# One hybrid recurrent and mixture-of-experts block: conditioning work dealt out anew, a norm in columns, other rounds of experts

## The chip, the cores and the metric

The kernel runs as one program on one core of a Trainium2 chip. A time is the device time of one execution in microseconds; where several were timed, the median stands. A profiled execution also gives a trace, whose times count from its first instruction (its span). In the trace PE is the matrix engine (PEld its weight loads), DVE the vector engine, ACT the scalar engine, POOL the general engine, and SP the engine whose queue issues the large loads. L12 is line 12 of the kernel's file.

## The reference, cut to what matters

One layer for 256 tokens of width 2048. A conditioning vector c gives six rows of 2048 (shift, scale and gate for each half), all by one product with w_ada:

```
mod = silu(c) @ w_ada + b_ada                       # (2048) x (2048, 12288), f32: 100 MB
sh1, sc1, g1, sh2, sc2, g2 = split(mod, 6)
x = x + g1 * mixer(rmsnorm(x) * (1 + sc1) + sh1)    # w_in 2048 x 6152, w_out 2048 x 2048
x = x + g2 * moe(rmsnorm(x) * (1 + sc2) + sh2)      # top 2 of 32 experts, each 3 x 4 MB
y = rmsnorm(x) * final_g
```

In the mixer, four mLSTM heads stand beside eight blocks of a linear recurrence. The recurrence's output `yr` is normed over each block of 128 channels: `yr * rsqrt(mean(yr*yr) + eps) * lru_norm_g`. In the experts' half a router picks a group and two experts for each token; each expert has a gate, an up and a down matrix of 4 MB each in f32. With the inputs that are timed, 512 places (256 tokens, two experts each) fall very unevenly on the experts: the fullest has 66, and six of the 32 have none, so that 26 experts are loaded, 312 chunks of 1 MB.

## The kernel before, in words

All weights stream through a ring of seven buffers of 1 MB (`ring`; one buffer of 128 partitions x 8 KB is a chunk). The function `chunk` takes the next buffer and issues its load on SP's queue. SP's and PE's instructions stand in the order in which the code is written; those of DVE and ACT are placed by a scheduler. A load into a buffer waits until the last reader of the buffer's former content is done.

The program has these stages. First two sections of the conditioning (`ada_now`) with the first products of w_in, then the remaining groups of w_in (`w_in_group`, for the gates, queries, keys, values and outputs), then w_out by token, then the routing, then the experts in ten rounds (`experts`), and an output stage. A product of w_in or w_out splits each chunk on ACT and DVE (`split`) into a high and a low part and multiplies in three passes on PE.

The four later sections of the conditioning (2, 4, 3 and 5, in this order, 16 chunks each) are read beside w_in and w_out. `between()` runs after each chunk of w_in and w_out: it takes one step of the side work and one more chunk of `ada_later`, sometimes two. The last six of the 64 chunks are read in the routing (`fill`). Each chunk is either multiplied on PE into the section's sum in PSUM, or multiplied and added on DVE into the tile `acc` (two instructions of 128 x 1024). `ON_PE` says which: of the sections 2, 4 and 3 the first three chunks, of section 5 all 16, 25 in total. `ada_sum` ends a section: PE adds up `acc` over its partitions (four products, 128 x 512 each), DVE adds the bias row.

The norm of the recurrence (`lru_norm`) squares on ACT, sums with a matrix of ones on PE, so that the sum stands in all 128 partitions, takes the root on ACT and the reciprocal on DVE over 128 x 512 elements, four times.

The experts' rounds: PE works with four column tiles of 32 tokens at once. An entry `(rank, tiles)` of `ROUNDS` is one expert, by its rank in fullness (30 and 31 are experts 0 and 1, known before the routing), and how many of the four tiles it takes. A round of two experts reads 24 chunks, one of four reads 48. PE does the same number of products in both. The loads of an expert without tokens are skipped, but its chunks still take their buffers in the ring. The ranks 24 and 25 have no tokens with these inputs. While the experts run, the ring has six more buffers, cut from tiles that are done with. The very first of them stands in the place of `acc`:

```
if count[0] in (1, 7):
    tag, bufs = ("acc", 1) if count[0] == 1 else ("ws", 3)
    ring.appendleft(st([128, 4, 512], f"more{count[0]}", tag, bufs))
```

So the first chunk of the first expert goes into `more1`, the old `acc`. Behind round `OVER_AFTER` (counted from 0) stands a loop for overfull experts (`overflow`). With these inputs it runs no times, but every engine meets at it; eight chunks of the next round are issued ahead of it (`PREFETCH`).

Of the kernel before, what the change touches and what calls it, by code (L numbers as in the profile page):

```python
# [13 lines left out]
AF = mybir.ActivationFunctionType  # L14
OP = mybir.AluOpType
# [3 lines left out]
S = 256  # L19
# [8 lines left out]

ROUNDS = [[(30, 2), (31, 2)], [(0, 3), (7, 1)], [(8, 1), (9, 1), (10, 1), (11, 1)], [(1, 3), (12, 1)],
          [(13, 1), (14, 1), (15, 1), (16, 1)], [(2, 3), (17, 1)], [(18, 1), (19, 1), (20, 1), (21, 1)],
          [(3, 2), (4, 2)], [(22, 1), (23, 1), (24, 1), (25, 1)], [(5, 2), (6, 2)]]
LAST = [26, 27, 28, 29]

OVER = [(30, 2), (31, 2), (0, 2), (1, 2), (2, 2)] + [(r, 1) for r in range(3, 15)]
CAP = {rank: 32 * tiles for members in ROUNDS for rank, tiles in members}
NR = len(ROUNDS)
NB = 1 + sum(n for _, n in OVER)
OVER_AFTER = 2  # L40

FILL = 3

# [1 line left out]

BESIDE = 53

ON_PE = {2: 3, 4: 3, 3: 3, 5: 16}

PREFETCH = 8  # L50

# [13 lines left out]
def constants():  # L65
# [20 lines left out]
    base, cap, osh = np.zeros(32), np.zeros(32), np.zeros(32)  # L86
    for r, members in enumerate(ROUNDS):
        col = 0
# [19 lines left out]
def block_kernel(ctx, tc, x, c, w_ada, b_ada, w_in, b_gates, vec_a, vec_b, w_lru_a, w_lru_x, w_out,  # L108
                 w_rt, b_rt, w_e_gate, w_e_up, w_e_down, const, out):
    nc = tc.nc  # L110
    V, A, G, PE, SP = nc.vector, nc.scalar, nc.gpsimd, nc.tensor, nc.sync
# [8 lines left out]
    def pb(shape=(128, 512), name="pb"):  # L120
        return psum.tile(list(shape), F32, name=name, tag="b", bufs=2)

    def w2(shape, name, dt=F32):
        return sb.tile(list(shape), dt, name=name, tag="w2", bufs=8)

    def st(shape, name, tag=None, bufs=1, dt=F32):
        return sb.tile(list(shape), dt, name=name, tag=tag or name, bufs=bufs)
# [4 lines left out]
    def tcopy(o, i):  # L132
        V.tensor_copy(o, i)
# [33 lines left out]
    ones = cs[:, C_ONE:C_ONE + 128]  # L167
# [31 lines left out]
    eps = epsc[:, 0:1]  # L199
# [6 lines left out]
    cz = st([128, 16, 36], "cz")  # L206
    V.memset(cz, 0.0)
    V.tensor_scalar(cz[:, :, 3], th, 0.5, None, op0=OP.mult)
    oz = cs[:, C_SEL + 8:C_SEL + 44]
    ada = st([128, 6, 16], "ada")  # L210
# [28 lines left out]

    acc = st([128, 4, 512], "acc")  # L240

    def ada_sum(sec, ps):
        yield
        if ON_PE[sec] < 16:
            for n in range(4):
                PE.matmul(ps[32 * n:32 * n + 32], oz[:, 3:35], acc[:, n], start=False, stop=True, skip_group_check=True)
        row = w2([128, 512], "row")
        V.tensor_tensor(row, ps, arow[sec], op=OP.add)
        yield
        one = 1.0 if sec in (1, 4) else 0.0  # L250
        for o, perm in ((ada[:, sec], False),) + (((adx[:, sec - 3], True),) if sec in (3, 4) else ()):
            pc = pb([128, 4, 4])
            for j in range(4):
                PE.matmul(pc[:, :, j], row[:, j::4] if perm else row[:, j * 128:j * 128 + 128],
                          ident[:, 0:128:32], start=True, stop=True)
            V.tensor_scalar(o, pc.rearrange("p a b -> p (a b)"), one, None, op0=OP.add)
            yield

    def ada_later():

        for sec in (2, 4, 3, 5):
            ada_start(sec, 32)
            ps = pa()
            pe = ON_PE[sec]
            for k in range(16):
                w = ada_row(sec, k)
                if k < pe:
                    for n in range(4):  # L270
                        PE.matmul(ps[32 * n:32 * n + 32], cz[:, k, 3:35], w[:, n], start=k == 0, stop=k == 15,
                                  skip_group_check=True)
                else:
                    for h in range(0, 4, 2):
                        o = acc[:, h:h + 2]
                        if k == pe:
                            V.tensor_scalar(o, w[:, h:h + 2], cz[:, k, 3:4], None, op0=OP.mult)
                        else:
                            V.scalar_tensor_tensor(o, w[:, h:h + 2], cz[:, k, 3:4], o, op0=OP.mult, op1=OP.add)  # L279
                if k == 15:  # L280
                    sums.append(ada_sum(sec, ps))
                yield

    later = ada_later()

    def bcast(cols):
        p = pb([128, 4, 128])
        for j in range(4):
            PE.transpose(p[:, j], cols[:, j:j + 1].to_broadcast([128, 128]), ident)  # L289
        return p.rearrange("p a b -> p (a b)")  # L290
# [46 lines left out]
    lng = lambda ch: col[:, 128 + ch:129 + ch]  # L337
# [178 lines left out]
    def lru_norm():  # L516
        sq = []
        for pair in range(4):
            a = XR[:, 2 * pair:2 * pair + 2]
            V.tensor_tensor(a, a, GR[:, 2 * pair:2 * pair + 2], op=OP.mult)  # L520
            sq.append(w2([128, 512], "sq"))
            A.activation(sq[-1], a.rearrange("p a b -> p (a b)"), AF.Square)
        yield
        for pair in range(4):
            pq = pb()
            PE.matmul(pq, ones, sq[pair], start=True, stop=True)
            A.activation(sq[pair], pq, AF.Sqrt, scale=1.0 / 128, bias=eps)
        yield
        for pair in range(4):
            V.reciprocal(sq[pair], sq[pair])  # L530
            for i, n in enumerate((2 * pair, 2 * pair + 1)):
                V.scalar_tensor_tensor(GR[:, n], XR[:, n], lng(n), sq[pair][:, i * S:i * S + S], op0=OP.mult, op1=OP.mult)
            yield

    def evac_qk(which, g):
# [29 lines left out]
    def values(hd):  # L565
        P = PT[hd]
        for t in range(2):
            po = pb([128, 257])
            for h in range(t + 1):
                lh = P[:, t * 128:t * 128 + 128] if h == 0 else P[:, 256:]  # L570
                PE.matmul(po, lh, va_aug[:, h, hd], start=h == 0, stop=h == t)
            i = hd * 2 + t
            tcopy(HR[:, t, hd], po[:, :256])
            tcopy(dn[:, 0, i:i + 1], po[:, 256:257])
            j = w2([128, 256], "tj")
            A.activation(j, HR[:, t, hd], AF.Square, accum_out=dn[:, 1, i:i + 1])
            tcopy(dn[:, 2, i:i + 1], gcols[:, 1, t, hd:hd + 1])
        yield
        if hd < 3:
            return  # L580
        V.tensor_scalar(dn[:, 3], dn[:, 0], -1.0, None, op0=OP.mult)
        V.tensor_tensor(dn[:, 0], dn[:, 0], dn[:, 3], op=OP.max)
        V.tensor_tensor(dn[:, 0], dn[:, 0], dn[:, 2], op=OP.max)
        V.reciprocal(dn[:, 0], dn[:, 0])
        V.tensor_tensor(dn[:, 1], dn[:, 1], dn[:, 0], op=OP.mult)
        V.tensor_tensor(dn[:, 1], dn[:, 1], dn[:, 0], op=OP.mult)
        A.activation(dn[:, 1], dn[:, 1], AF.Sqrt, scale=1.0 / 256, bias=eps)
        V.reciprocal(dn[:, 1], dn[:, 1])
        V.tensor_tensor(dn[:, 0], dn[:, 0], dn[:, 1], op=OP.mult)
        for i in range(8):  # L590
            V.tensor_scalar(HR[:, i % 2, i // 2], HR[:, i % 2, i // 2], dn[:, 0, i:i + 1], None, op0=OP.mult)
# [20 lines left out]
    for sec in (1, 0):  # L612
        ps = pb()
# [51 lines left out]
    XR, GR = XG[:, 0], XG[:, 1]  # L665
# [16 lines left out]
    for g in range(2):  # L682
        ps = [pa() for _ in range(2)]
        for kk in range(4):
            w = chunk(w_in[kk * 512:kk * 512 + 512, 2048 + g * 512:2560 + g * 512]
                      .rearrange("(k p) n -> p k n", p=128))
# [4 lines left out]
    HR = XR.rearrange("p (t h a) s -> p t h (a s)", t=2, h=4)  # L691
# [38 lines left out]
    def router(n):  # L730
        yield
        xts = []
        for i in range(2):
            p = pb([128, 2, S])
            xt = w2([128, 2, S], "xt")
            k = n * 4 + i * 2
            for j in range(2):
                for h in range(2):
                    PE.transpose(p[:, j, h * 128:h * 128 + 128], X1[:, h, (k + j) * 128:(k + j + 1) * 128], ident)
            V.tensor_tensor(xt, p, ada[:, 4, k:k + 2, None].to_broadcast([128, 2, S]), op=OP.mult)  # L740
            xts.append(xt)
            yield
        for i in range(2):
            for j in range(2):
                k = n * 4 + i * 2 + j
                for h in range(2):
                    PE.matmul(plg[:, h], xts[i][:, j, h * 128:h * 128 + 128], wr[:, k], start=k == 0 and h == 0,
                              stop=k == 15, skip_group_check=True)
# [18 lines left out]
    ps = [[pa() for _ in range(2)] for _ in range(2)]  # L767
# [14 lines left out]
    for n in (2, 3):  # L782
        ps = [pa() for _ in range(2)]
# [326 lines left out]
    def members_of(r):  # L1110
        ms, c0 = [], 0
        for rank, tiles in ROUNDS[r]:
            if rank >= 30:
# [94 lines left out]
    for r in range(NR):  # L1208
# [8 lines left out]
        if not last:  # L1217
            Cw = spread_of(r + 1)
            ms = members_of(r + 1)
        if r == OVER_AFTER:  # L1220
            flush()
# [57 lines left out]
```

## Time and profile before

| | |
|---|---|
| median of three runs | 1365.17 us (1364.59 to 1368.4) |
| profiled execution: its own time, its span | 1366.29 us, 1364.4 us |
| PE busy | 1179.1 us (86%) |
| DVE busy | 553.5 us (41%) |
| ACT busy | 348.1 us (26%) |
| moved on SP's queue (q1) | 500.11 MB, 91.8% of 16 engines' span |
| mean granted TensorE clock | 0.956 |

The profiled execution took 1.1 us longer than the median; 1.9 us of its own time lie outside its span. A share over the whole span mixes stages with different limits, so stages are read one by one below. The DMA share of a stretch is the mean busy share of the core's 16 DMA engines.

### The profile page before, as it was taken

The page shows a single profiled execution, that of the slowest core. Times are in us where ns is not written, and L with a number is a line of the kernel's source. Part 1 is how long each engine was busy: PE and PEld are TensorE (multiplying, and loading weights), DVE is VectorE, ACT ScalarE, POOL GpSimd, SP SyncE. Part 2 cuts the span into 40 slices and gives each one's busy share as a digit, 9 for nine tenths or more (in the row PEclk, how much of TensorE's full clock was granted, in tenths as well). Part 3 has the DMA queues.
Part 4 walks back from the last instruction along what each step waited for, and adds up shares of the span by engine and source line. Part 5 has one row for each costly group of instructions (what it writes and reads, how often), then busy time and mean ns, then how long its engine had stood idle before and what let it go on. Part 6 is the DMA issues. An engine that isn't in the chain of part 4 may idle for free. (4 is left out here: it accounts for less than half of the span.)

```text
span 1364.4 us, 20209 instructions
## 1 busy us (share of the span) xinstructions
PE 1179.1 (86%) x8178; PEld 674.6 (49%) x8178; DVE 553.5 (41%) x999; ACT 348.1 (26%) x543; POOL 3.5 (0%) x10
## 2 busy tenths in 40 slices
PE   4888999899999999899987859867789777989986
PEld 0567888788789777534421313313134113343432
DVE  1333679989859943523230130310122201313314
ACT  2332595635435423421100100100001001010103
POOL 0000000000000000000000000000000000000000
PEclk9999999999999999799998989998899888999998
DMA  9999768778969966999999999999999999999995
GB/s 340 367 374 362 260 255 328 281 265 342 387 244 364 388 256 254 414 364 394 424 424 424 424 391 374 424 425 425 425 425 425 425 425 424 425 424 418 365 420 224
DMA packets 116896, 504.82 MB, mean 370 GB/s; under 512 B 12424, under 2 KB 14760, under 8 KB 69184
## 3 DMA queue, kind: packets, MB, share of 16 engines
q1 hardware_dynamic: 115264, 500.11, 91.8%
q0 software_dynamic: 288, 2.10, 0.4%
q8 instruction: 65, 1.06, 0.3%
q10 hardware_dynamic: 1248, 1.29, 0.3%
q14 instruction: 31, 0.25, 0.0%
HBM read 526.54 MB, written 2.10 MB: 387 GB/s over the span
## 5 line engine op out<-in xcount | busy, mean ns | idle before, releaser
L1026 PE MATMUL pa<-ring,XE 128*32 128x512 f32 x1336 | 269.4, 632 | 41.6 <-DMA ring<-in_w_e_up_dram 26.5
L1026 PE MATMUL pa<-more,XE 128*32 128x512 f32 x1224 | 235.1, 632 | 42.5 <-DMA more<-in_w_e_up_dram 23.0
L434 PE MATMUL pa<-HH,ws 128*128 128x256 f32 x640 | 185.7, 290 | 10.7 <-DVE ws L417 10.7
L432 PE MATMUL pa<-HH,ws 128*128 128x256 f32 x640 | 188.5, 295 | 3.6 <-ACT ws L416 1.9
L433 PE MATMUL pa<-HL,ws 128*128 128x256 f32 x640 | 185.1, 289 | 1.4 <-DVE HL L327 1.4
L416 ACT ACTIVATE ws<-ring 128x1024 fp32r<-128x1024 f32 x128 | 134.6, 1059 | 185.3 <-PE pa L434 94.7
L417 DVE TENSOR_TENSOR ws<-ring,ws 128x1024 fp32r<-128x1024 f32 x128 | 154.4, 1218 | 58.2 <-ACT ws L416 57.6
L1026 PEld LDWEIGHTS pa<-ring,XE 128*32 128x32 f32 x1336 | 66.4, 114 | 172.1 <-issue 89.5
L432 PEld LDWEIGHTS pa<-HH,ws 128*128 128x128 f32 x640 | 126.4, 198 | 15.8 <-issue 6.5
L1026 PEld LDWEIGHTS pa<-more,XE 128*32 128x32 f32 x1224 | 57.5, 115 | 153.0 <-issue 82.5
L434 PEld LDWEIGHTS pa<-HH,ws 128*128 128x128 f32 x640 | 126.4, 197 | 12.7 <-DVE ws L417 12.6
L433 PEld LDWEIGHTS pa<-HL,ws 128*128 128x128 f32 x640 | 126.6, 198 | 2.3 <-DVE HL L327 1.9
L1081 PE MATMUL pa<-ring,hT 128*32 128x512 f32 x616 | 110.5, 607 | 11.4 <-DMA ring<-in_w_e_down_dram 11.4
L897 ACT ACTIVATE XE<-pb,adx 128x128 f32<-128x128 f32 x80 | 36.6, 458 | 297.4 <-DVE XE L900 297.4
L1081 PE MATMUL pa<-more,hT 128*32 128x512 f32 x536 | 98.4, 619 | 14.0 <-DMA more<-in_w_e_down_dram 14.0
L1058 DVE TENSOR_TENSOR hs<-hs,pa 128x512 f32<-128x512 f32 x10 | 6.9, 688 | 240.8 <-PE pa L1026 240.8
L1046 DVE TENSOR_TENSOR X<-X,pa 128x512 f32<-128x512 f32 x80 | 51.8, 682 | 112.0 <-PE pa L1044 112.0
L279 DVE SCALAR_TENSOR_TENSOR acc<-ring,cz,acc 128x1024 f32<-128x1024 f32 x72 | 90.1, 1272 | 0.0
L893 PE MATMUL pb<-two,XN 128*128 128x128 f32 x640 | 80.7, 286 | 8.0 <-ACT hT L1065 6.7
L893 PEld LDWEIGHTS pb<-two,XN 128*128 128x128 f32 x640 | 76.4, 199 | 19.6 <-issue 9.4
L1037 ACT ACTIVATE ys<-y 128x512 fp32r<-128x512 f32 x40 | 25.2, 630 | 186.9 <-DVE y L1035 186.9
L900 DVE TENSOR_SCALAR XE<-pb,adx 128x128 f32<-128x128 f32 x80 | 32.8, 410 | 71.8 <-PE pb L893 51.2
(361 smaller groups left out, 1161.4 us busy)
## 6 DMA issues: line engine op xcount, KB each, us to landing
ring<-in_w_ada_dram SPq DMA_DIRECT2D x96, 1024.0 KB, 8.4
ring<-in_w_e_up_dram SPq DMA_DIRECT2D x63, 1024.0 KB, 19.6
ring<-in_w_e_down_dram SPq DMA_DIRECT2D x61, 1024.0 KB, 19.6
more<-in_w_e_gate_dram SPq DMA_DIRECT2D x56, 1024.0 KB, 17.8
ring<-in_w_e_gate_dram SPq DMA_DIRECT2D x56, 1024.0 KB, 16.8
more<-in_w_e_down_dram SPq DMA_DIRECT2D x51, 1024.0 KB, 19.6
more<-in_w_e_up_dram SPq DMA_DIRECT2D x49, 1024.0 KB, 19.5
ring<-in_w_in_dram SPq DMA_DIRECT2D x48, 1024.0 KB, 6.8
```

The lines of the kernel that those rows point to most:

```text
L279: V.scalar_tensor_tensor(o, w[:, h:h + 2], cz[:, k, 3:4], o, op0=OP.mult, op1=OP.add)
L416: A.activation(ws[:, 0], s, AF.Copy)
L417: V.tensor_tensor(ws[:, 1], s, ws[:, 0], op=OP.subtract)
L432: PE.matmul(o, wh[:, cc], HH[:, k], start=k == 0 and ch % 2 == 0, stop=False, skip_group_check=True)
L433: PE.matmul(o, wh[:, cc], HL[:, k], start=False, stop=False, skip_group_check=True)
L434: PE.matmul(o, wl[:, cc], HH[:, k], start=False, stop=k == 15, skip_group_check=True)
L893: PE.matmul(p[:, j], XN[:, h, kk, j], which[:, h], start=h == 0, stop=h == 1)
L897: A.activation(XE[:, k], p[:, j], AF.Identity, scale=adx[:, 1, k:k + 1], bias=adx[:, 0, k:k + 1])
L900: V.tensor_scalar(XE[:, k], p[:, j], adx[:, 1, k:k + 1], adx[:, 0, k:k + 1], op0=OP.mult, op1=OP.add)
L1026: PE.matmul(o[c0:c0 + width], lhs(kk, j)[:, c0:c0 + width], w[:, j], start=first and j == 0, stop=last and j == 3)
L1046: V.tensor_tensor(X1[:, h, ns], X1[:, h, ns], pc, op=OP.add)
L1081: PE.matmul(pds[n][c0:c0 + width], hT[:, f, c0:c0 + width], w[:, n], start=f == 0, stop=f == 3)
```

## The change

Five edits. First, `ON_PE` becomes a set of places among the 64 later conditioning chunks: 20 go to PE (nine of section 2, three of section 4, one of section 3, and of section 5 its first and the last six), 44 to DVE. Every section now has a part in `acc`, section 5 too. Second, the sum over `acc` is held in a list and given out either in `ada_sum` or before the next section's first write to `acc`, whichever comes first in the code. Third, `lru_norm` sums the squares as 16 products with one column, takes root and reciprocal over 128 x 16, and spreads the result with 16 transposes (`bcast`). Fourth, two pieces of DVE's work go to ACT: the copy of the heads' values out of PSUM, and the scaling of the transposed `X1` for the router. Fifth, `ROUNDS` has two rounds of four experts and four of three in place of four of four, and the overflow loop stands behind the sixth round in place of the third.

```
+ROUNDS: ... [(1, 3), (12, 1)],
-          [(13, 1), (14, 1), (15, 1), (16, 1)], [(2, 3), (17, 1)], [(18, 1), (19, 1), (20, 1), (21, 1)],
-          [(3, 2), (4, 2)], [(22, 1), (23, 1), (24, 1), (25, 1)], [(5, 2), (6, 2)]]
+          [(3, 2), (13, 1), (22, 1)], [(2, 3), (14, 1)], [(15, 1), (16, 1), (17, 1), (18, 1)],
+          [(5, 2), (19, 1), (24, 1)], [(4, 2), (20, 1), (23, 1)], [(6, 2), (21, 1), (25, 1)]]
-OVER_AFTER = 2
+OVER_AFTER = 5
-ON_PE = {2: 3, 4: 3, 3: 3, 5: 16}
+ON_PE = {0, 1, 2, 3, 5, 7, 10, 12, 14, 16, 19, 22, 32, 48, 58, 59, 60, 61, 62, 63}
+    unsummed = []
+    def acc_sum():
+        if unsummed:
+            ps, begun = unsummed.pop()
+            for n in range(4):
+                PE.matmul(ps[32 * n:32 * n + 32], oz[:, 3:35], acc[:, n], start=not begun, stop=True, ...)
     def ada_sum(sec, ps):
         yield
-        if ON_PE[sec] < 16:
-            for n in range(4): PE.matmul(ps[...], oz[:, 3:35], acc[:, n], start=False, stop=True, ...)
+        acc_sum()
...
-        for sec in (2, 4, 3, 5):
+        for i, sec in enumerate((2, 4, 3, 5)):
-                if k < pe:
+                if 16 * i + k in ON_PE:
                     ... four products on PE
                 else:
+                    acc_sum()
                     ... two instructions on DVE into acc
                 if k == 15:
+                    if summed:
+                        unsummed.append((ps, begun))
                     sums.append(ada_sum(sec, ps))
... lru_norm
+        pq = pb([128, 8, 2])
+        for n in range(8):
+            for h in range(2):
+                PE.matmul(pq[:, n, h:h + 1], sq[n // 2][:, c0:c0 + 128], ones[:, 0:1], start=True, stop=True)
+        A.activation(rr, pq.rearrange("p n h -> p (n h)"), AF.Sqrt, scale=1.0 / 128, bias=eps)
+        V.reciprocal(rr, rr)
         for pair in range(4):
-            PE.matmul(pq, ones, sq[pair], start=True, stop=True)
-            A.activation(sq[pair], pq, AF.Sqrt, scale=1.0 / 128, bias=eps)
-            V.reciprocal(sq[pair], sq[pair])
+            rb = bcast(rr[:, 4 * pair:4 * pair + 4])
... values
-            tcopy(HR[:, t, hd], po[:, :256])
+            A.activation(HR[:, t, hd], po[:, :256], AF.Copy)
... router
-            V.tensor_tensor(xt, p, ada[:, 4, k:k + 2, None].to_broadcast([128, 2, S]), op=OP.mult)
+            for j in range(2):
+                A.activation(xt[:, j], p[:, j], AF.Copy, scale=ada[:, 4, k + j:k + j + 1])
```

The first place is SP's queue at the seam between the last conditioning chunk (into `ring_68`) and the first expert's chunks; `more_4675` and `more_4701` are `more1`. The names in brackets are the semaphores that a load waits for: DMAHW for earlier loads, PE and DVE for those engines. Before:

```order
L156 DMA ring_67<-in_w_ada_dram 128x2048 [waits DMAHW6_49,PE_49]
L156 DMA ring_68<-in_w_ada_dram 128x2048 [waits DMAHW7_49,DVE_49]
L156 DMA more_4675<-in_w_e_gate_dram 128x2048
L156 DMA ring_69<-in_w_e_gate_dram 128x2048 [waits DMAHW0_49,PE_49]
L156 DMA more_4707<-in_w_e_gate_dram 128x2048 [waits DMAHW1_49]
```

And in the changed kernel:

```order
L158 DMA ring_67<-in_w_ada_dram 128x2048 [waits DMAHW6_49,DVE_49]
L158 DMA ring_68<-in_w_ada_dram 128x2048 [waits DMAHW7_49,DVE_49]
L158 DMA more_4701<-in_w_e_gate_dram 128x2048 [waits PE_49]
L158 DMA ring_69<-in_w_e_gate_dram 128x2048 [waits DMAHW0_49]
L158 DMA more_4733<-in_w_e_gate_dram 128x2048 [waits DMAHW1_49]
```

The load into `more1` waited for nothing before and now waits for PE; the load behind it has lost its own wait for PE.

The second place is PE at the end of the routing: counts and prefix sums, the first gather for experts 0 and 1 (`two`, `XN`), the expert table (`hot`), the last two conditioning chunks, the end of section 5 (`row`) and the second gather. Before:

```order
L937 MATMUL pb<-cmp,cs 32x32
L893 MATMUL pb<-two,XN 128x128 x8
L943 MATMUL pb<-hot,cs 128x32 x3
L271 MATMUL pa<-ring_67,cz 32x512 x4
L271 MATMUL pa<-ring_68,cz 32x512 x4
L254 MATMUL pb<-cs,row 128x4 x4
L893 MATMUL pb<-two,XN 128x128 x8
```

And in the changed kernel:

```order
L958 MATMUL pb<-cmp,cs 32x32
L914 MATMUL pb<-two,XN 128x128 x8
L964 MATMUL pb<-hot,cs 128x32 x3
L281 MATMUL pa<-ring_67,cz 32x512 x4
L281 MATMUL pa<-ring_68,cz 32x512 x4
L251 MATMUL pa<-acc,cs 32x512 x4
L264 MATMUL pb<-cs,row 128x4 x4
```

New is the sum over `acc` for section 5, which stands behind the first gather and the last two conditioning chunks.

The third place is ACT ahead of the routing: the squares of the last quarter of `X1` (`t`, `ss`), the root for the norm (`r`), and the scaled `X1` for the gathers (`XN`). Before:

```order
L728 ACTIVATE t_4416,ss_3635<-X_3827 128x512
L728 ACTIVATE t_4420,ss_3635<-X_3827 128x512
L295 ACT_TABLE_LOAD
L295 ACTIVATE r_4468<-ssum,epsc 128x2
L875 ACTIVATE XN<-X_3827,r_4468 128x512 x8
```

And in the changed kernel:

```order
L748 ACTIVATE t_4436,ss_3667<-X_3859 128x512
L748 ACTIVATE t_4440,ss_3667<-X_3859 128x512
L761 ACTIVATE xt<-pb,ada 128x256 x2
L310 ACT_TABLE_LOAD
L310 ACTIVATE r_4490<-ssum,epsc 128x2
L761 ACTIVATE xt<-pb,ada 128x256 x2
L896 ACTIVATE XN<-X_3859,r_4490 128x512 x8
```

The router's last four scalings, which DVE did, now stand on ACT around the root.

## Rows read from the trace of the kernel before

**Rows 1.** The page's 40 equal slices of the span: GB/s moved.

```profile
GB/s 340 367 374 362 260 255 328 281 265 342 387 244 364 388 256 254 414 364 394 424 424 424 424 391 374 424 425 425 425 425 425 425 425 424 425 424 418 365 420 224
```

**Rows 2.** Stages: us, busy PE, PEld, DVE, ACT, POOL, PE clock, DMA share, GB/s.

```profile
136.00:546.00 410.00, 394.49 (x2601) 337.24 (x2600) 319.69 (x426) 207.30 (x297) 2.77 (x5) 0.98 0.81 302
546.00:582.00 36.00, 30.19 (x175) 19.45 (x177) 18.24 (x92) 15.35 (x21) 0.00 (x0) 0.76 1.01 416
582.00:640.00 58.00, 57.11 (x514) 25.83 (x510) 13.31 (x75) 12.26 (x23) 0.00 (x0) 1.00 0.93 371
640.00:810.00 170.00, 140.14 (x944) 50.58 (x936) 41.12 (x89) 15.78 (x30) 0.00 (x0) 0.94 1.01 425
810.00:830.00 20.00, 11.89 (x88) 3.20 (x92) 3.01 (x8) 0.00 (x0) 0.00 (x0) 0.67 0.70 280
830.00:1260.00 430.00, 355.92 (x2482) 131.01 (x2474) 84.82 (x180) 36.89 (x71) 0.00 (x0) 0.95 1.01 424
1260.00:1294.00 34.00, 31.64 (x268) 14.65 (x266) 9.23 (x17) 6.66 (x13) 0.00 (x0) 1.00 0.91 365
```

**Rows 3.** A stretch of w_in and that of w_out, columns as above.

```profile
239.00:273.00 34.00, 27.89 (x217) 26.82 (x217) 33.62 (x53) 21.72 (x30) 0.00 (x0) 0.96 0.79 282
443.00:546.00 103.00, 102.87 (x529) 77.78 (x528) 61.22 (x71) 36.61 (x47) 1.19 (x2) 0.98 0.79 299
```

**Rows 4.** Longest wait of PE in 205 to 275: total us, times, longest.

```profile
PE pa L434 <- DVE ws L417: 4.9, 3, 2.6
```

**Rows 5.** Groups by line and shape: busy us, mean ns, idle before.

```profile
L279 DVE SCALAR_TENSOR_TENSOR acc<-ring,cz,acc 128x1024 f32<-128x1024 f32 x72 | 90.1, 1272 | 0.0
L271 PE MATMUL pa<-ring,cz 128*32 128x512 f32 x200 | 27.8, 645 | 0.0
L530 DVE RECIPROCAL sq<-sq 128x512 f32<-128x512 f32 x4 | 13.4, 3348 | 0.4 <-ACT sq L527 0.4
L233 PE MATMUL pb<-cs,row 128*128 128x1 f32 x64 | 9.8, 274 | 2.5 <-DVE row L228 2.5
L289 PE MATMUL pb<-cs,ada 128*128 128x128 f32 x32 | 4.7, 280 | 0.0
L526 PE MATMUL pb<-sq,cs 128*128 128x512 f32 x8 | 3.9, 605 | 1.4 <-ACT sq L527 1.4
L319 ACT ACTIVATE xT<-pb,ada 128x256 f32<-128x256 f32 x16 | 6.7, 470 | 47.7 <-PE pb L317 47.7
```

**Rows 6.** The sums over `acc`: first and last start.

```profile
L246 PE MATMUL pa<-acc,cs x24: 592/605/618, 291.3 to 475.3; 128*32 128x512 f32 x24
```

**Rows 7.** SP's issues in order of time: start, us, load, count.

```profile
521.63 23.00 SPq L156 DMA_DIRECT2D ring<-in_w_ada_dram  x7
544.67 0.42 SPq L156 DMA_DIRECT2D more<-in_w_e_gate_dram  x1
```

**Rows 8.** PE in order of time at the end of the routing.

```profile
569.69 3.64 PE L271 MATMUL pa<-ring,cz 128*32 128x512 f32 x16
...
579.64 1.07 PE L1026 MATMUL pa<-more,XE 128*32 128x512 f32 x2
```

**Rows 9.** ACT and DVE in order of time ahead of the routing.

```profile
552.53 1.28 ACT L295 ACT_TABLE_LOAD   x1
553.82 0.30 ACT L295 ACTIVATE r<-ssum,epsc 128x2 f32<-128x2 f32 x1
...
555.83 0.42 DVE L808 SCALAR_TENSOR_TENSOR lg<-pa,r,shw 128x36 f32<-128x36 f32 x2 [1.10 <-PE pa L747]
```

**Rows 10.** PE in order of time at the third round's end and behind the loop.

```profile
797.91 0.62 PE L1081 MATMUL pa<-more,hT 128*32 128x512 f32 x1 [1.91 <-DMA more<-in_w_e_down_dram]
...
818.11 6.21 PE L1026 MATMUL pa<-more,XE 128*32 128x512 f32 x32 [8.17 <-SPq L1152]
```

**Rows 11.** The chain that ended last: a two-expert round's up load and down products.

```profile
1002.49 21.06 DMA more<-in_w_e_up_dram
...
1038.06 7.05 PE pa L1081 x64
```

More of the change, by code (lines that the diff above doesn't have):

```diff
@@ L240, in block_kernel @@
     acc = st([128, 4, 512], "acc")
+    unsummed = []
[3 more added lines that the diff above has]
+            for n in range(4):
+                PE.matmul(ps[32 * n:32 * n + 32], oz[:, 3:35], acc[:, n], start=not begun, stop=True,
+                          skip_group_check=True)
     def ada_sum(sec, ps):
         yield
-        if ON_PE[sec] < 16:
-            for n in range(4):
-                PE.matmul(ps[32 * n:32 * n + 32], oz[:, 3:35], acc[:, n], start=False, stop=True, skip_group_check=True)
+        acc_sum()
         row = w2([128, 512], "row")
@@ L259, in ada_later @@
     def ada_later():
-        for sec in (2, 4, 3, 5):
+        for i, sec in enumerate((2, 4, 3, 5)):
             ada_start(sec, 32)
             ps = pa()
-            pe = ON_PE[sec]
+            begun = summed = False
             for k in range(16):
                 w = ada_row(sec, k)
-                if k < pe:
+                if 16 * i + k in ON_PE:
                     for n in range(4):
-                        PE.matmul(ps[32 * n:32 * n + 32], cz[:, k, 3:35], w[:, n], start=k == 0, stop=k == 15,
+                        PE.matmul(ps[32 * n:32 * n + 32], cz[:, k, 3:35], w[:, n], start=not begun, stop=False,
                                   skip_group_check=True)
+                    begun = True
                 else:
+                    acc_sum()
                     for h in range(0, 4, 2):
                         o = acc[:, h:h + 2]
-                        if k == pe:
+                        if not summed:
                             V.tensor_scalar(o, w[:, h:h + 2], cz[:, k, 3:4], None, op0=OP.mult)
@@ L279, in ada_later @@
                             V.scalar_tensor_tensor(o, w[:, h:h + 2], cz[:, k, 3:4], o, op0=OP.mult, op1=OP.add)
+                    summed = True
                 if k == 15:
+                    if summed:
+                        unsummed.append((ps, begun))
                     sums.append(ada_sum(sec, ps))
@@ L523, in lru_norm @@
         yield
-        for pair in range(4):
-            pq = pb()
-            PE.matmul(pq, ones, sq[pair], start=True, stop=True)
-            A.activation(sq[pair], pq, AF.Sqrt, scale=1.0 / 128, bias=eps)
+        pq = pb([128, 8, 2])
+        for n in range(8):
+            for h in range(2):
+                c0 = n % 2 * S + h * 128
+                PE.matmul(pq[:, n, h:h + 1], sq[n // 2][:, c0:c0 + 128], ones[:, 0:1], start=True, stop=True)
+        rr = st([128, 16], "rr")
+        A.activation(rr, pq.rearrange("p n h -> p (n h)"), AF.Sqrt, scale=1.0 / 128, bias=eps)
+        V.reciprocal(rr, rr)
         yield
         for pair in range(4):
-            V.reciprocal(sq[pair], sq[pair])
+            rb = bcast(rr[:, 4 * pair:4 * pair + 4])
             for i, n in enumerate((2 * pair, 2 * pair + 1)):
-                V.scalar_tensor_tensor(GR[:, n], XR[:, n], lng(n), sq[pair][:, i * S:i * S + S], op0=OP.mult, op1=OP.mult)
+                V.scalar_tensor_tensor(GR[:, n], XR[:, n], lng(n), rb[:, i * S:i * S + S], op0=OP.mult, op1=OP.mult)
             yield
```

## Prediction

> **What bounds the kernel now.** I read the page's slices first. From about 650 us on nearly every slice moves 424 to 425 GB/s, and before that 244 to 414 [rows 1]: two halves with two limits. The table by stages shows both. In the experts' rounds the DMA share is 1.01 at 424 to 425 GB/s in 640 to 810 and in 830 to 1260, while PE is busy for 140 of 170 and 356 of 430 us [rows 2]. So the experts are bound by their bytes: 312 chunks of 1.05 MB at 424 GB/s are 2.47 us each, 772 us, and a time without transfers there lengthens the run by just that time. Three stretches lose transfers: 582 to 640 runs at 371 GB/s, which is 58 x (1 - 371/424) = 7.3 us lost; 810 to 830, at the loop, at 280, 6.8 us; 1260 to 1294 at 365, 4.7 us [rows 2]. In the first and the last PE is busy without a break (57 of 58 and 32 of 34 us): the buffers are full and SP waits for PE.
>
> In w_in and w_out (136 to 546) PE is busy 394.5 of 410 us while the DMA share is 0.81 [rows 2]. There PE is the limit, 15.5 us of it idle, and DVE is nearly full in one part: 33.62 of 34 us in 239 to 273, where PE falls to 27.89 [rows 3] and waits for DVE's half of a split (4.9 us) [rows 4]. Between the two halves lies the seam, and it decides this case.
>
> **The change part by part.**
>
> *Work in w_in and w_out.* A conditioning chunk costs PE 27.8 / 25 = 1.11 us [rows 5]. 25 become 20, and the five that go all lie in this stage: -5.6 us. The norm drops four products (3.9 us) and adds 16 products of one column and 16 transposes. The nearest rows for those are the 32 products of one column (64 records, 9.8 us: 0.306 each, so 4.9) and the transposes (0.147 each, so 2.35) [rows 5]: +3.3 us. On DVE four reciprocals go, 13.4 us, and in the section that lies beside them six chunks of 2 x 1.27 us go to PE, 15.3 us [rows 5]. That is 28.7 us fewer in the stretch that was full, so most of PE's wait there should end. I take -5 us of idle; the bounds are 0, and -9 (the 6.1 us idle in 239 to 273 and a third of the other 9.4). DVE takes on nine chunks of section 5 beside w_out, 22.9 us, where it is busy 61 of 103 us now [rows 3], so there is room. Stage sum: -5.6 + 3.3 - 5 = **-7.3 us**, bounds -11.3 and 0, the upper one if the norm's new transposes wait for DVE to free their PSUM buffer as long as the old waits did.
>
> The copies that go from DVE to ACT I cost at nothing here: ACT is busy 207 of 410 us [rows 2], and PE doesn't wait for DVE in w_out, where it is busy 102.9 of 103 [rows 3].
>
> *Routing.* The router's scalings now stand on ACT, the first pair behind the squares and the second behind a table load and the root. Before, the table load started at 552.53 and `lg` at 555.83 [rows 9]. Now: 552.5 + 0.94 for a pair at 0.47 [rows 5] + 1.28 + 0.30 [rows 9] + 0.94 = 556.0, then the router's products, for which `lg` waited 1.1 us before [rows 9]: `lg` at 557.1, **+1.3 us** for all that hangs on the routing (bounds 0 and 2.5).
>
> The Trainium skill (ScalarE: Activation LUTs, What ACT_TABLE_LOAD costs) adds a drain of about 1380 ns to each table load of 1283 ns. This trace shows the load at 1.28 us with the root 0.01 us behind it [rows 9] and no such gap; by the page the routing term would be 2.7 us.
>
> *The seam.* This is the large term. Before, the last sum over `acc` started at 475.3 us [rows 6], long before the first expert's chunk, which goes into the same place, was issued at 544.67, right behind the last conditioning chunks (seven issues from 521.63 to 544.63) [rows 7]. From there on DMA ran at 416 GB/s through the routing [rows 2]: the experts' weights were fetched while PE routed. In the changed kernel section 5 has a part in `acc`, and its sum stands on PE behind the first gather and behind the last two conditioning products (the second place of the order above). The load into `more1` waits for it (the first place). The issues of [rows 7] come in the order of the code: behind the waiting load stand all other expert chunks, also those into buffers that are free. So nothing is issued for the whole routing.
>
> When is the sum done? The last two conditioning products end at 569.69 + 3.64 = 573.33 [rows 8]; the sum has the shape of a chunk's products, 1.1 us; with the routing's 1.3 that is 575.7. When does DMA run dry? At 544.63 + 2.5 = 547.1, a chunk's time behind the last issue; the delay from issue to data is the same at both ends and cancels. The pause is 575.7 - 547.1 = **+28.6 us**. Both ends move together with the stage ahead. Bounds: 26 (no routing delay, the last issue's data late by 1.3) and 31.
>
> The Trainium skill's rule on this (Perfetto Trace Analysis, DMA Instruction, HWDGE) says that the issuing sequencer itself sits in the semaphore wait, and is free for the next instruction only when the descriptors are made. By it the whole queue is held. If a queue let later loads pass, 12 chunks into other buffers would fill the pause and the term would be near 0. No row here shows a load passing another.
>
> What comes back: with the experts' loads 28.6 us late, PE waits for chunks instead of SP for buffers, so the 7.3 us lost in 582 to 640 are not lost again: **-7.3 us** (bounds -7.3 and -5). PE itself starts the experts hardly later (579.64 before [rows 8]; now two chunks after 575.7 + 1.2, near 582), but 24 chunks are 59 us of DMA, and the lead of full buffers with which PE entered the first round of four is gone.
>
> *Rounds and loop.* All 26 experts are loaded in either order, so bytes don't change. The loop moves behind a round of two. In the third round PE waited for the last down chunk (1.91 us, 797.91) and started again at 818.11 behind the loop [rows 10]. Behind a round of two PE is later against its loads: the last up chunk landed at 1023.55, the eight down chunks are 19.8 us, to 1043.3, and the down products ran without a wait from 1038.06 for 13.9 us, to 1051.9 [rows 11]. That is 8.6 us behind the last landing; in the third round 801.5 - 797.9 = 3.6. The eight chunks issued ahead cover as much as before, so the loop's 6.8 us grow by up to 5: **+4 us** (bounds 0 and 6).
>
> The 4.7 us in 1260 to 1294 come where three rounds with two loaded experts follow each other, in one of which half of the buffers are given to experts without tokens. Now the ninth round loads three, and no round loses more than a third: **-4.7 us** (bounds -4.7 and 0).
>
> *Sum.* -7.3 + 28.6 - 7.3 + 4 - 4.7 = +13.3 us on the profiled execution's own time, 1366.3 (span 1364.4 and 1.9 around it): 1379.6. The median is 1.1 lower, so **1379 us**, 1.0% slower. All bounds one way give -11.3 + 26 - 7.3 + 0 - 4.7 = +2.7, the other way 0 + 31 - 5 + 6 - 0 = +32.
>
> **Rivals.**
>
> *Faster: the load is not held.* If the sum over `acc` were done by 547, the pause is 0, the 7.3 us are lost as before, and -7.3 + 4 - 4.7 = -8 gives 1357. For it: the edit says that sums are given out early. Against it: early means before the next section, and section 5 has none behind it; its sum stands behind the routing's gather. It decides from a release before about 555. Chance 0.03.
>
> *Absorbed, no change.* If the first rounds were bound by PE so far that only PE's start counts (+2.3 us, 579.64 to 582), the sum is -7.3 + 2.3 + 4 - 4.7 = -5.7 at the lowest, and about 1365 with half of the pause kept. For it: PE is busy 57 of 58 us in the first round [rows 2]. Against it: from the third round on transfers run at full rate [rows 2], so late bytes stay late. Chance 0.05.
>
> *Slower still: DVE falls behind in w_out.* It has 44 chunks and stands in order behind residual sums that wait for PE. If it holds splits or ring buffers there, the stage gains nothing and may lose 5 us: 1386 to 1391. For it: DVE was the limit in 239 to 273 [rows 3]. Against it: 61 of 103 us busy [rows 3]. Chance 0.15.
>
> **How the numbers follow.** The forecast, a full pause with the gains beside it, has 0.77; its own range is 1370 to 1388. The range for all reaches to the DVE case above and to the small end of the bounds below: 1368 to 1391. A change of under 0.3% (4.1 us) can't be told from none. Slower: 0.77 + 0.15 = 0.92; same 0.05; faster 0.03.
>
> **What the profile after would show.** DMA share near 0 for some 28 us just ahead of the experts' first products, with SP waiting there for PE at the sum over `acc`; PE waiting for DMA in the first two rounds, and no stretch under 420 GB/s in them; the seam about 7 us earlier; PE's wait for DVE near 240 us gone; the loop's gap at 9 to 12 us. Wrong would be: expert chunks landing during the routing, a seam at or after 546, or a gap in the last rounds.

## The result, and the profile after

The changed kernel takes 1374.68 us (median of four executions, 1374.03 to 1376.22), the kernel before 1365.72 us on the same chip (four, 1364.59 to 1368.4). The ratio is 1.0064, with a 95% interval of 1.0047 to 1.0082: 9 us slower, where 1379 us were forecast. The profiled execution took 1376.22 us, its span is 1374.4 us, against 1366.29 and 1364.4 before: +9.9 and +10.0.

The page's slices of GB/s after, the row that answers to [rows 1]:

```profile
GB/s 337 373 376 359 268 231 324 264 310 328 384 268 348 378 323 212 184 425 424 424 425 425 425 425 424 424 425 424 424 425 299 425 423 426 423 424 426 425 416 217
```

A slice is 34.4 us. Where the row of before has 254, 414, 364 and 394 at the seam, this one has 212 and 184, then full rate from the eighteenth slice on. The dip to 391 and 374 in the middle (the loop) has become one to 299, in the thirty-first slice instead of the twenty-fourth and twenty-fifth, and the dip to 365 near the end is gone. The windows give the sizes; columns as in [rows 2]:

```profile
136.00:273.00 137.00, 133.29 (x1060) 119.83 (x1059) 97.12 (x146) 86.63 (x125) 0.53 (x1) 0.96 0.75 271
239.00:273.00 34.00, 33.93 (x281) 30.62 (x280) 26.80 (x50) 21.20 (x28) 0.00 (x0) 1.00 0.66 247
443.00:510.00 67.00, 66.87 (x326) 54.20 (x325) 57.14 (x65) 30.31 (x43) 1.19 (x2) 0.97 0.91 344
546.00:576.00 30.00, 21.89 (x139) 14.05 (x141) 14.23 (x84) 13.14 (x17) 0.00 (x0) 0.77 0.24 96
576.00:640.00 64.00, 60.98 (x530) 27.04 (x526) 14.35 (x76) 12.26 (x23) 0.00 (x0) 1.00 1.01 424
810.00:1030.00 220.00, 192.03 (x1442) 77.71 (x1434) 57.20 (x118) 23.67 (x45) 0.00 (x0) 0.97 1.01 424
1030.00:1050.00 20.00, 13.32 (x72) 5.26 (x70) 6.36 (x18) 0.63 (x1) 0.00 (x0) 0.66 0.52 209
1050.00:1340.00 290.00, 231.34 (x1598) 85.07 (x1598) 50.70 (x105) 22.54 (x44) 0.00 (x0) 0.95 1.01 424
```

In 239 to 273 PE is now the full engine and DVE is not, the reverse of [rows 3]. The routing moves 96 GB/s where it moved 416. Behind it no slice falls under 423 GB/s but the loop's and the last two.

SP's issues in order of time (start, us, load, count), to set beside [rows 7]:

```profile
513.34 21.31 SPq L158 DMA_DIRECT2D ring<-in_w_ada_dram  x7
567.64 0.33 SPq L158 DMA_DIRECT2D more<-in_w_e_gate_dram  x1
568.02 0.42 SPq L158 DMA_DIRECT2D ring<-in_w_e_gate_dram  x1
```

The last conditioning chunk is issued at 513.34 + 21.31 = 534.65, 10.0 us earlier than before. The next issue, into `more1`, comes 33.0 us later; before, it came 0.04 us later. The list of SP's waits (total us, times, longest) puts this on the sum over `acc`, L251:

```profile
SPq L158 <- PE pa L251: 33.0, 1, 33.0
```

The load behind it goes into a free ring buffer and starts only when the one ahead has gone. PE's part of this, at the end of the routing, beside [rows 8]:

```profile
552.92 0.84 PE L930 MATMUL pcnt<-MS,cs 128*128 128x32 f32 x4 [2.26 <-DVE MS L888]
...
562.87 3.64 PE L281 MATMUL pa<-ring,cz 128*32 128x512 f32 x16
566.29 1.28 PE L251 MATMUL pa<-acc,cs 128*32 128x512 f32 x8
...
572.50 1.05 PE L1047 MATMUL pa<-more,XE 128*32 128x512 f32 x4 [1.10 <-DMA more<-in_w_e_gate_dram]
```

The sum over `acc` (L251) ends at 567.57 and SP issues at 567.64. The first expert products then wait for DMA, which did not happen in [rows 8].

ACT and DVE ahead of the routing, beside [rows 9]:

```profile
544.06 1.28 ACT L310 ACT_TABLE_LOAD   x1
545.36 0.30 ACT L310 ACTIVATE r<-ssum,epsc 128x2 f32<-128x2 f32 x1
...
547.99 0.42 DVE L829 SCALAR_TENSOR_TENSOR lg<-pa,r,shw 128x36 f32<-128x36 f32 x2 [2.14 <-PE pa L768]
```

And PE's groups by shape from 136 to 600 us, beside [rows 5]: the chunks on PE, the norm's products of one column, and its transposes.

```profile
L281 PE MATMUL pa<-ring,cz 128*32 128x512 f32 x160 | 23.3, 671 | 0.0
L544 PE MATMUL pb<-cs,sq 128*128 128x1 f32 x32 | 4.5, 276 | 0.0
L304 PE MATMUL pb<-cs,rr 128*128 128x128 f32 x16 | 2.4, 271 | 0.0
```

### The profile page after: what moved, and what is told of

Read it like the earlier page. It is cut to its first block, busy times and chain, and to the rows that moved or that the text cites. A ratio compares the mean times of both kernels' runs of the same rounds, so it can differ in the third digit from the quotient of the medians.

```text
span 1374.4 us, 20213 instructions
## 1 busy us (share of the span) xinstructions
PE 1183.6 (86%) x8186; PEld 683.3 (50%) x8186; DVE 545.6 (40%) x990; ACT 352.0 (26%) x562; POOL 4.0 (0%) x10
## 5 line engine op out<-in xcount | busy, mean ns | idle before, releaser
L1047 PE MATMUL pa<-ring,XE 128*32 128x512 f32 x1368 | 278.6, 636 | 49.2 <-DMA ring<-in_w_e_up_dram 24.5
L1047 PE MATMUL pa<-more,XE 128*32 128x512 f32 x1192 | 250.7, 631 | 50.4 <-DMA more<-in_w_e_up_dram 37.2
L1047 PEld LDWEIGHTS pa<-ring,XE 128*32 128x32 f32 x1368 | 69.9, 115 | 175.2 <-issue 85.0
L1047 PEld LDWEIGHTS pa<-more,XE 128*32 128x32 f32 x1192 | 61.4, 114 | 168.7 <-issue 73.9
L1102 PE MATMUL pa<-more,hT 128*32 128x512 f32 x528 | 103.5, 609 | 8.3 <-DMA more<-in_w_e_down_dram 8.3
L291 DVE SCALAR_TENSOR_TENSOR acc<-ring,cz,acc 128x1024 f32<-128x1024 f32 x80 | 100.2, 1275 | 0.6 <-DMA ring<-in_w_ada_dram 0.6
L1058 ACT ACTIVATE ys<-y 128x512 fp32r<-128x512 f32 x40 | 25.2, 630 | 179.1 <-DVE y L1056 179.1
```

Of the source, the lines that this page charges most:

```text
L1047: PE.matmul(o[c0:c0 + width], lhs(kk, j)[:, c0:c0 + width], w[:, j], start=first and j == 0, stop=last and j == 3)
L1102: PE.matmul(pds[n][c0:c0 + width], hT[:, f, c0:c0 + width], w[:, n], start=f == 0, stop=f == 3)
```

## The experiments

The theory: SP's queue is held at the load into `more1` until section 5's sum over `acc` is done, and the bytes not moved meanwhile come back only in part. The rivals: the time goes to the new places of the chunks (DVE falling behind), to the new norm, or to the new rounds and the loop's place. Every ratio is to the kernel before on the same chip, whose medians were 1365.5, 1366.0 and 1364.8 us in the three groups of runs.

### late_acc: `acc` joins the ring last

Nothing of the work changes; the old `acc` becomes the thirteenth buffer in place of the eighth, so the load that needs it stands further back in SP's queue.

```
-                if count[0] in (1, 7):
-                    tag, bufs = ("acc", 1) if count[0] == 1 else ("ws", 3)
+                if count[0] in (6, 13):
+                    tag, bufs = ("acc", 1) if count[0] == 13 else ("ws", 3)
...
-                if count[0] in (3, 5):
+                if count[0] in (2, 4):
```

> The changed kernel, but the tile that once was acc joins the ring as the 13th buffer for expert chunks in place of the first. Theory A, the held queue: SP's wait for the last sum over acc no longer stands ahead of the experts' loads, the 30.5 us without issues (534.7 to 567.6) shrink to under 8, and the 7 us in which SP waits for full buffers in the first round come back: 1374.7 - 30.5 + 7.3 and 0 to 5 for what is left of the pause, 1351 to 1357 us. Theory B, the slowdown comes from the rounds and the loop, and the pause is mostly absorbed: 1368 or more.

Measured: 1355.22 us (1351.92 to 1356.18), ratio 0.9917 [0.9901, 0.9933]. SP's issues, PE's first expert products, and the seam's windows of this kernel:

```profile
535.83 0.42 SPq L158 DMA_DIRECT2D ring<-in_w_e_gate_dram  x1
...
568.74 0.33 SPq L158 DMA_DIRECT2D more<-in_w_e_up_dram  x1
```

```profile
572.44 0.62 PE L1047 MATMUL pa<-ring,XE 128*32 128x512 f32 x2
```

```profile
530.00:570.00 40.00, 33.19 (x176) 22.43 (x175) 20.04 (x89) 17.66 (x25) 0.00 (x0) 0.79 0.87 358
570.00:640.00 70.00, 69.11 (x604) 31.46 (x603) 21.11 (x97) 14.43 (x27) 0.00 (x0) 1.00 0.95 380
```

The load into the same ring buffer (now the first expert chunk, in the changed kernel the second) stood waiting until 568.02 and starts at 535.83 when the blocked one is not ahead of it. The load into `acc` still goes out only at 568.74, but for another reason. SP's waits from 540 to 640 (total us, times, longest):

```profile
SPq L158 <- PE pa L281: 22.8, 6, 13.9
SPq L158 <- PE pa L251: 0.5, 1, 0.5
```

The longest is for PE's last conditioning products (L281), whose ring buffers come ahead of `acc` in the queue; for the sum itself (L251) SP waits 0.5 us. In 530 to 570, 40 x (1 - 358/424) = 6.2 us are lost, and 7.3 in the next 70, as in [rows 2]. PE reaches the experts at 572.44, as in the changed kernel at 572.50: PE's start is the same in both, and the runs differ by 19.5 us. That refutes the rival that only PE's start counts. The theory holds, and this kernel beats both.

### before_late_acc: the control

The same edit on the kernel before, where the load into the old `acc` did not wait.

> The control to late_acc: the kernel before, with the buffer acc moved from the first place behind the ring to the thirteenth. Theory A (late_acc gained only because it took away a pause that the change had brought; the kernel before has no such pause, 544.63 to 544.67 us): same as before within 3 us, 1363 to 1368. Rival B (the order of buffers is worth something by itself): 1352 to 1360.

Measured: 1365.96 us (1363.04 to 1368.27), ratio 1.0003 [0.9992, 1.0014]. That is theory A: in the kernel before, the order of the buffers by itself is worth nothing, so late_acc's 19.5 us are the removed wait.

### seam_only: the change's wait alone

The kernel before, written with places, and one chunk of section 5 (place 49) given to `acc`, so that its sum is needed at the end; norm, copies and rounds are those of before.

```
-ON_PE = {2: 3, 4: 3, 3: 3, 5: 16}
+ON_PE = {0, 1, 2, 16, 17, 18, 32, 33, 34, 48, *range(50, 64)}
```

> The kernel before with one thing of the change: one chunk of section 5 (its second) goes to acc on DVE, so that section 5 ends with a sum over acc, by the new code for the sums; all else, norm, copies, rounds, loop, as before. Theory A: the queue is held for about 30 us at the seam, 7 of them come back: 1365.7 + 30 - 7.3 - 1 = 1385 to 1390 us, slower than the changed kernel itself. Theory B, absorbed: under 1372.

Measured: 1382.83 us (1380.61 to 1383.66), ratio 1.0119 [1.0102, 1.0135]: 17.3 us slower. SP's issues, then PE's last two conditioning chunks and the clock there, in this kernel:

```profile
522.08 22.99 SPq L156 DMA_DIRECT2D ring<-in_w_ada_dram  x7
572.75 0.33 SPq L156 DMA_DIRECT2D more<-in_w_e_gate_dram  x1
```

```profile
569.91 1.92 PE L279 MATMUL pa<-ring,cz 128*32 128x512 f32 x16
```

```profile
565.00:575.00 10.00, 8.34 (x58) 6.10 (x59) 7.02 (x42) 1.74 (x5) 0.00 (x0) 0.81 0.12 31
```

One dependence, on work that costs a microsecond, makes the kernel slower by more than the whole change does. The time lies under the 1385 to 1390 us expected. The pause is 572.75 - 545.07 - 2.5 = 25.2 us and not 30, and 25.2 less the 7.3 that come back are 17.9. A part of the difference is PE's clock: the same eight products (16 records, two to a product) take 1.92 us here and 3.64 in the changed kernel, whose granted clock (next to last column but one) over the like ten microseconds is 0.51, near the lower of the two levels:

```profile
557.00:567.00 10.00, 9.23 (x46) 5.83 (x46) 5.60 (x37) 1.36 (x5) 0.00 (x0) 0.51 0.01 2
```

So the pause has the clock of the routing in it, which is not the same in every kernel.

### old_places: the change without section 5's part in `acc`

```
-ON_PE = {0, 1, 2, 3, 5, 7, 10, 12, 14, 16, 19, 22, 32, 48, 58, 59, 60, 61, 62, 63}
+ON_PE = {0, 1, 2, 16, 17, 18, 32, 33, 34, *range(48, 64)}
```

> The changed kernel with the conditioning chunks on PE that were there before (25; section 5 wholly on PE, so no sum over acc at its end). Theory A: no pause, SP issues the first expert chunk at once: 1374.7 - 30.5 + 7.3 = 1351.5, and up to 9 us back because PE has five more chunks (5.6) and DVE is fuller in the first section: 1352 to 1361 us. Theory B: 1370 or more.

Measured: 1355.99 us (1352.41 to 1358.38), ratio 0.9933 [0.9919, 0.9946]. SP's issues:

```profile
514.94 22.99 SPq L158 DMA_DIRECT2D ring<-in_w_ada_dram  x7
537.98 0.43 SPq L158 DMA_DIRECT2D more<-in_w_e_gate_dram  x1
```

No pause, and the time of late_acc by another way. The conditioning chunks end at 537.93, 3.3 us later than in the changed kernel: so much of the stage's 10.0 us is the new places', on top of norm and copies. In the seam that gain costs six times its size.

### early_sum: the wait is kept, its release is moved

The last two conditioning chunks and the sum stand ahead of the routing's counts (`FILL = 7` in place of 3).

> The changed kernel with the last two conditioning chunks and the sum over acc of section 5 ahead of the routing's counts on PE (seven steps in place of three there); the first expert chunk still goes into acc. Theory A, the held queue: SP is let go when the sum ends, near 553 in place of 567.6, so the pause falls from 30.5 to 16 us and the time by 14.5, less 0 to 3 for waits on full buffers that come back: 1360 to 1363 us. Theory B, the pause doesn't set the time: 1372 to 1376.

Measured: 1361.67 us (1359.35 to 1362.35), ratio 0.9966 [0.9953, 0.9979]. SP's issues:

```profile
514.46 21.31 SPq L158 DMA_DIRECT2D ring<-in_w_ada_dram  x7
553.55 0.33 SPq L158 DMA_DIRECT2D more<-in_w_e_gate_dram  x1
```

The release comes 14.1 us earlier and the time falls by 13.0. The pause is paid nearly one for one as long as it is there.

### late_acc_early: both

> Both cures together: acc joins the ring as the 13th buffer, and the last two chunks and the sum stand ahead of the counts. Theory A: the 6 us that the kernel with acc as the 13th buffer alone still lost in 560 to 580, where SP waited for the buffers of the last two conditioning chunks, go; 4.6 us of full buffers in 580 to 640 may grow by up to 3: 1355.2 - 6 + 0 to 3, 1349 to 1353 us. If those waits only move, 1354 to 1356.

Measured: 1356.12 us (1354.12 to 1357.91), ratio 0.9931 [0.9918, 0.9944], the time of late_acc; the gain that I expected is not there. SP's issues show why:

```profile
555.65 0.33 SPq L158 DMA_DIRECT2D more<-in_w_e_up_dram  x1
576.07 0.33 SPq L158 DMA_DIRECT2D ring<-in_w_e_up_dram  x1
```

The load into `acc` goes out 13.1 us earlier than in late_acc (568.74), but the load behind it waits to 576.07, in late_acc to 576.11. All thirteen buffers are full by then, and the next comes free only with PE's first expert products. Behind that point an earlier release buys nothing in this kernel.

### old_rounds: rounds and loop of before in the changed kernel

`ROUNDS` and `OVER_AFTER = 2` of before.

> The changed kernel with the rounds and the place of the loop as before. Theory A: these two edits are worth +3.3 (the loop's gap 10.1 in place of 6.8 us) and -4.7 (the gap near 1270), so undoing them gives 1374 to 1378 us, the pause unchanged. Theory B, the slowdown is theirs: 1368 or less.

Measured: 1380.05 us (1378.9 to 1380.41), ratio 1.0103 [1.0087, 1.0118], 5.4 us over the changed kernel and over the 1374 to 1378 expected. Its windows at the loop and at the three rounds near the end:

```profile
820.00:840.00 20.00, 12.42 (x76) 5.35 (x79) 5.04 (x16) 0.00 (x0) 0.00 (x0) 0.61 0.56 219
1280.00:1300.00 20.00, 19.11 (x176) 9.58 (x178) 4.03 (x9) 4.77 (x10) 0.00 (x0) 1.00 0.80 317
```

The gap of 1260 to 1294 in [rows 2] is back, with 20 x (1 - 317/424) = 5.0 us, and the new rounds take it away. But the loop, behind its old place, loses 9.7 us here and not 6.8: the 3.3 us that I expected back did not come.

### loop_third: the loop alone at its old place

`OVER_AFTER = 2`, with the new rounds. The third round has four experts, in the kernel before as here; the sixth, behind which the changed kernel has its loop, has two.

> The changed kernel with the loop behind the third round, as before; the rounds are the new ones. Prediction's working: the loop costs 6.8 us behind a round of four and 10.1 behind a round of two, so 1370 to 1373 us. Rival: what the loop costs depends on how late the loads are, not on the round's kind (with the old rounds and the pause it lost 9.7 us behind the third), so 1374 to 1376.

Measured: 1375.28 us (1374.45 to 1376.85), ratio 1.0072 [1.0059, 1.0085]: the changed kernel's time, and the rival's 1374 to 1376, not the 1370 to 1373 of the prediction's working. Its window at the loop:

```profile
820.00:840.00 20.00, 12.48 (x92) 5.63 (x94) 4.84 (x15) 0.00 (x0) 0.00 (x0) 0.70 0.56 221
```

9.6 us are lost behind the third round, a round of four, and 10.1 behind the sixth, a round of two. The loop's place is not what made its loss grow. What is left between this kernel and old_rounds is the rounds alone: 4.8 us by the medians, 4.2 by the ratios.

### late_acc_loop_third: the same in the best kernel

> late_acc with the loop behind the third round instead of the sixth. Theory A (the loop costs 8.5 to 10 us of loads wherever it stands): 1353 to 1357, a single loss of 8 to 10 us near 820 us and none near 1010. Rival B (behind the third round the buffers hold more, as in the kernel before, which lost 6.8 there): 1350 to 1353.

Measured: 1353.41 us (1351.05 to 1354.49), ratio 0.9909 [0.9893, 0.9926], the same as late_acc within the intervals, and at the lower edge of theory A. Its window at the loop:

```profile
800.00:820.00 20.00, 13.65 (x100) 3.54 (x104) 1.25 (x5) 0.00 (x0) 0.00 (x0) 0.69 0.64 252
```

8.1 us lost, late_acc 8.7 at the sixth round (240 GB/s in 1010 to 1030). Without the pause the loss is smaller by some 1.5 us, but it is not back at 6.8, and the spread of one execution is of that size.

### old_norm: the norm of before in the changed kernel

```
-                PE.matmul(pq[:, n, h:h + 1], sq[n // 2][:, c0:c0 + 128], ones[:, 0:1], start=True, stop=True)
...
+        for pair in range(4):
+            PE.matmul(pq, ones, sq[pair], start=True, stop=True)
+            A.activation(sq[pair], pq, AF.Sqrt, scale=1.0 / 128, bias=eps)
...
+            V.reciprocal(sq[pair], sq[pair])
```

> The changed kernel with the norm of the recurrence as before (sum in all partitions, reciprocals over 128 x 512). Prediction's working: PE is spared 3.0 us, DVE gets 13 us more in 205 to 273, where it is now busy 50 of 68 us, so at most some 2 to 5 us of PE's waits come back: 1372 to 1377 us. Rival, the reciprocals alone had filled DVE: the 7.5 us of PE idle come back in full, 1378 or more.

Measured: 1375.09 us (1372.42 to 1378.22), ratio 1.0068 [1.0052, 1.0083], as the changed kernel. A stretch of w_in in four kernels, in this order: before, old_places (new norm, old places), old_norm (old norm, new places) and the changed kernel (both new). Then SP's last conditioning issues in old_norm:

```profile
205.00:273.00 68.00, 60.46 (x498) 55.72 (x497) 66.68 (x89) 39.86 (x51) 0.00 (x0) 0.98 0.82 304
205.00:273.00 68.00, 64.35 (x570) 62.27 (x569) 63.95 (x93) 36.68 (x47) 0.00 (x0) 1.00 0.87 329
205.00:273.00 68.00, 65.90 (x555) 57.63 (x554) 57.81 (x81) 40.72 (x51) 0.00 (x0) 1.00 0.81 303
205.00:273.00 68.00, 67.93 (x572) 61.86 (x572) 49.86 (x77) 34.58 (x44) 0.00 (x0) 0.95 0.78 293
```

```profile
513.42 21.31 SPq L158 DMA_DIRECT2D ring<-in_w_ada_dram  x7
```

The old norm spares PE 3.0 us of products, and the stage still ends 0.1 us later: over all of it (136 to 534.7) PE is idle for 10.75 us, in the changed kernel for 7.88. With the chunks placed anew the norm in columns is worth nothing; with the old places (old_places) norm and copies alone brought the seam forward by 6.7 us (544.63 to 537.93). In 205 to 273 PE was idle for 7.5 us before; the new norm with the old places leaves 3.7, the new places with the old norm 2.1, both 0.1. The two edits share most of one wait, so what the norm still ends behind the new places only pays its own products. No run has the copies alone.

## Why the prediction was right

The forecast was slower, by the queue held at `more1`, and that is what the runs show: seam_only brings the wait alone (+17.3 us), late_acc takes it alone away (-19.5), before_late_acc excludes the order of buffers. Step by step:

- **The queue is held.** Right. The load behind `more1` had a free buffer and moved from 568.02 to 535.83 when it stood ahead of the waiting one. What the Trainium skill states (Perfetto Trace Analysis, DMA Instruction, HWDGE), that the issuing sequencer itself sits in the semaphore wait, agrees with this, as far as these rows go.
- **Stage: -7.3 forecast, -10.0 measured** (544.63 to 534.65). The norm's products came out near their price: 4.5 + 2.4 us of new ones less 3.9 are +3.0, forecast +3.3. That PE's clock fell beside and behind them was not in the forecast (last section). Mis-sized was the wait that ends: PE's idle time in 205 to 273 fell from 7.5 us to 0.1 (the rows in the section on old_norm), in the whole stage from 15.5 to 7.9, so about 7.5 in place of the 5 taken. I chose a middle value where the stretch's limit goes away altogether.
- **Routing: +1.3 forecast, +1.4 measured** from w_out's last product (549.82 before, 540.56 after) to the first counts (560.76 and 552.92). The first pair of scalings holds the table load back and the second stands behind the root, as forecast. No drain stands behind the table load: the root starts 0.02 us after it. Nor would one have changed this term, since both kernels have the load there.
- **Pause: 28.6 forecast, 567.64 - 534.65 - 2.5 = 30.5 measured.** Besides the 1.4 above, w_out's end moved only 9.3 of the 10.0 us, and the counts to the last chunks' products took 9.95 us (552.92 to 562.87) in place of 8.93 (560.76 to 569.69): the granted clock was already 0.53 in 553 to 555, where the same work before (561 to 563) had 1.00.
- **What comes back: -7.3, measured the same.** 576 to 640 runs at 424 GB/s.
- **Loop: +4 forecast, 20 x (1 - 209/424) = 10.1 us lost, so +3.3, but for a reason that falls.** I put it on the round of two ahead of the loop; loop_third and old_rounds lose 9.6 and 9.7 us behind the third round, a round of four. That the size fitted was luck. seam_only, with the same pause but norm and places of before, lost 7.6 at its loop, so the pause alone does not make it either. What does stays open.
- **Rounds: -4.7 forecast, gap gone.** Right: old_rounds, which undoes the loop's place too, is 5.4 us slower, and the rounds alone (old_rounds against loop_third) make 4.8.

The measured terms give -10.0 + 30.5 - 7.3 + 3.3 - 4.7 = +11.8 on a span that grew 10.0; the 1.8 us that are left are not placed, and executions of one kernel differ by as much. Against +13.3 forecast the largest miss is the stage's, -2.7 us; the pause missed by +1.9 the other way, so a part of the two cancels, which is luck as well.

Of the rivals, "faster" and "absorbed" needed an early release or a start of PE that decides; early_sum and late_acc show where those would have led. "DVE falls behind" did not come: it was busy 57.14 of 67 us in 443 to 510, with PE at 66.87. That leaves the change as two good parts (stage -10, rounds -5) and a loop that loses 3 more, under one dependence of +20 (1.0064 - 0.9917 = 1.47%).

## What to carry to other kernels

A buffer that is reused as a load target inherits every later use of its old content: before giving a tile new work late in a stage, look where its place comes up in the load queue, since in SP's queue here one waiting load stopped all that followed, free buffers or not (535.83 against 568.02). Put the buffer that comes free last at the place in the queue that is reached last; that turned +9 us into -10 here, at no cost. Two edits that relieve the same engine need not add up (7.5 us of idle ended by both here, 3.9 and 5.4 by each alone), so cost the second one on what the first leaves.

## What the runs showed of the hardware that was not expected

The granted clock in the routing differed between kernels that do the same work there: 0.51 in 557 to 567 us of the changed kernel, 0.81 in 565 to 575 of seam_only, and the same eight products took 3.64 and 1.92 us. Read in steps of 2 us, the clock stood at its lower level (0.50) from 554 to 566 in the changed kernel, from 562 to 568 in seam_only and from 564 to 580 in the kernel before. Ahead of it PE did much alike in the first two: 3.67 of 4 us busy (547 to 551) and 2.96 of 3 (556 to 559) at a granted clock of 1.00 beside the routing's first chunks, then 2.87 and 2.57 of 5 us in the counts (from 552 and from 560), at 0.61 and 0.69. No run here says which difference decides.

The granted clock also fell where no term had it: at the norm in columns. PE's products of one column, first in the changed kernel and then in old_places, and the windows of 232 to 240 in the changed kernel, in old_places and in old_norm:

```profile
229.80 4.55 PE L544 MATMUL pb<-cs,sq 128*128 128x1 f32 x32
```

```profile
226.58 3.63 PE L544 MATMUL pb<-cs,sq 128*128 128x1 f32 x32
```

```profile
232.00:240.00 8.00, 8.00 (x43) 8.00 (x43) 5.42 (x10) 3.54 (x7) 0.00 (x0) 0.57 0.85 340
232.00:240.00 8.00, 8.00 (x69) 8.00 (x69) 6.59 (x13) 4.65 (x9) 0.00 (x0) 1.00 0.32 101
232.00:240.00 8.00, 6.57 (x42) 5.06 (x41) 8.00 (x8) 7.93 (x11) 0.00 (x0) 1.00 0.96 383
```

In the changed kernel the granted clock was 1.00 up to 232 and stood at its lower level (0.50) from 234 to 239, beside the last of these products and behind them, with PE busy throughout. The 22 records of w_in's products that follow took 4.8 us; at their spacing before the fall (0.12 us) they would have taken 2.6, so about 2.2 us were lost, an estimate. All seven kernels with the new norm and the new places show this fall. In old_places the clock stayed at 1.00 behind the same products, and why is open. The kernel before has a fall of its own, 0.79 in 268 to 276, where the changed kernel has 1.00; so the sum of the stage doesn't show the loss.

The loop that runs no times costs the load queue 6.8 to 10.3 us in every kernel of this study (10.3 in old_norm), behind the third round as behind the sixth, while eight chunks issued ahead stand for 19.8 us of transfers.
